# A planner's choice of engine for the query and key scaling, and 96 more constant bytes, in a one-core decoder layer

## The chip, the cores and the metric

The kernel runs on one core of one Trainium2 chip. The time is that of one execution on the device, in microseconds (us), first instruction to last with the launch around it; smaller is better. The engines are named as the profile names them: PE is TensorE's matmuls, PEld its loading of weights (the stationary operand), DVE is VectorE, ACT is ScalarE, POOL is GpSimd, SP the engine that only issues DMAs here.

## The reference, cut to what matters

One decoder layer on 1024 tokens of width 1024, all float32. Half of the mixer is stick-breaking attention (8 heads of 64), half a convolution; a gated feed-forward network follows.

```python
h = rms_norm(x, norm1_g)
q, k, v, glu_a, glu_b = split(h @ w_in)            # 5 x 512 columns
q = rms_norm(q.reshape(1, S, 8, 64), q_norm_g)     # each head's 64 values by themselves
k = rms_norm(k.reshape(1, S, 8, 64), k_norm_g)
attn = stick_breaking_attention(q, k, v)
c = causal_depthwise_conv(glu_a * sigmoid(glu_b), conv_dw_w, conv_dw_b)   # width 31
c = silu(layer_norm(c))
x = x + concat([attn, c]) @ w_out
h = rms_norm(x, norm2_g)
gate, val = split(h @ w_up)                        # 2 x 2816 columns
x = x + (silu(causal_dwconv3(gate)) * val) @ w_down
```

The diff touches the line `q = rms_norm(...)` and the one for `k`: for each token and head, 64 values are squared and summed, `rs` is the inverse root of their mean, and the 64 values are multiplied by `rs`. The gains are applied later.

## The kernel before, in words

**Precision.** Each large product is made of float32r operands split in a high and a low part: `mm3` (lines 324 to 327) issues three matmuls, high by high, high by low, low by high. The first operand of each is the stationary one (PEld loads 128 columns of it, 512 bytes in each partition), the second streams 512 columns past it.

**Stages.** First come the input projections, with the convolution and the attention beside them (one plan, lines 385 to 1409, up to about 437 us). Then the output projection's attention half, the second norm and the operands of the feed-forward network (a second plan, up to about 490 us). Then the up-projection: `up(f, A)` for 22 slices f of 128 channels, in one level of a Strassen-like scheme of seven products of 12 matmuls each (lines 1674 to 1700, 490 to 917 us). Last the down-projection `dn` (line 1844, 917 us to the end).

**Who sets the order.** `Plan` is a list scheduler written in Python that runs while the kernel is built. Each operation is added with a cost in ns for its engine, a due time (`key`), the operations that it comes after, and the buffer slots ("tokens") that it takes. `Plan.run` repeatedly takes the operation that can start first; then `in_order` makes each engine execute in exactly that order. So an engine waits in order: a late operation holds all that is queued behind it. If an operation's cost is given for several engines (a dict), the plan takes the engine on which it would end first: `start + cost`, where start is the later of its inputs and of the engine's being free. Key "DVE2" stands for DVE, and says that the operation shares a memory port with POOL: then the cost grows by as much as POOL's running operation holds on, at most by its own cost, and a POOL operation that runs beside it is put off likewise. Plain "DVE" costs know nothing of POOL.

**The operations around the change.** `project("qk0_", ...)` makes the queries and keys of heads 0 to 3, tile t of 128 tokens after tile t: 24 matmuls into a PSUM bank, 256 query and 256 key columns. `summed` (line 557) does the rest, for all eight tiles (`SUMMED_FIRST`), and for tiles 6 and 7 of heads 4 to 7 (`SUMMED`; tiles 4 and 5 there go through `normalized`, line 533):

1. copy out of PSUM on ACT or DVE (`copy_out`, line 528),
2. square on ACT (line 568),
3. sum over each 64 on DVE (line 577),
4. `rstd` on POOL (two small operations, lines 316 and 317),
5. `scale` on DVE: `tensor_tensor` with `rs` broadcast over 64 columns (line 573), two instructions of 128x256 for heads 0 to 3, one of 128x512 for heads 4 to 7. Its planned cost is 750.

`normalized` scales on ACT instead, in eight `activation` instructions of 128x64 each (line 547). `queries_keys` (tiles 0 to 3 of heads 4 to 7) scales out of PSUM on DVE, line 998; the diff leaves both alone.

**The convolution beside it.** For each of four channel groups c, DVE runs 31 dependent taps, one instruction each (`conv_a`, line 694, then `conv_b`, line 704). ACT makes 15 more scaled terms (line 718) that POOL adds up one after the other (line 721, three terms ahead at most). Three DVE operations (lines 734 to 736) join the three sums. When all four groups are joined (`conv_done`), PE turns them for the layer norm (`ln`, line 757), and those transposes stand in PE's queue between the query and key products. `double` (the queries' copy for the attention) waits for `conv_done` and for all eight scales.

**The next projection.** Tiles 4 to 7 of heads 4 to 7 use four pairs of weight rows `w_qk`. Each is loaded into one of two `raw` slots, copied to its high part on ACT (`hi_qk`, line 479), and subtracted for its low part on DVE or POOL (`lo_qk`, line 483). The parts lie in eight `whl` slots, six of which the weights of `qk0_` hold until the last tile has used them.

**Memory.** Pools without `side` are laid from the low end of each partition, those with `side="right"` from the high end. Low: the constants (`cst`, of which the unused tile `pad` is the first), small statistics, `mixp` (the convolution's sums, later the attention's result and the gates), `qkvp`, `convp`, and in the later stages `op` (tags xt, h2, v, m, t). High: weights (`whl`, `raw`), `h`, keys, the operands `b` of the up-projection, and all operands of the down-projection. In the kernel before, the large low tiles begin at 128 bytes past a multiple of 256, the high ones at 224, save two of the four `pad` tiles that hold the first weights of `glu` and `qk0_` (96). In the up-projection, the stationary operands of products 11 and 22 are low tiles (`op`, tags v and m; for f = 0, 11 and 12 in `mixp`), those of 12, S1, S2, S3, S4 high ones (`whl`); all moving operands are high.

Of the kernel before, what the change touches and what calls it, by code (L numbers as in the profile page):

```python
# [8 lines left out]
F32 = mybir.dt.float32  # L9
F32R = mybir.dt.float32r  # L10
BF16 = mybir.dt.bfloat16
AF = mybir.ActivationFunctionType
# [4 lines left out]
P = 128  # L17
# [45 lines left out]
class Plan:  # L63
# [32 lines left out]
    def add(self, cost, *args):  # L96
        if not isinstance(cost, dict):
            cost, args = {cost: args[0]}, (lambda eng, f=args[1]: f(),) + args[2:]
        op = Plan.Op()
        op.shares = "DVE2" in cost  # L100
        op.cost, op.emit, op.key = {e.rstrip("2"): c for e, c in cost.items()}, args[0], args[1]
        op.after = list(args[2]) if len(args) > 2 else []
        op.takes = list(args[3]) if len(args) > 3 else []
        op.end, op.engine, op.n, op.kb, op.dmas = None, None, len(self.ops), 512, 1
        self.ops.append(op)
        return op
# [101 lines left out]
def kernel(  # L208
# [21 lines left out]
    nc = tc.nc  # L230
# [28 lines left out]
    def const(shape, dt, name):  # L259
        return cst.tile(shape, dt, tag=name, name=name)  # L260


    const([P, 8], F32, "pad")

    small = ctx.enter_context(tc.tile_pool(name="small", bufs=1))
    mix_ctx = ExitStack()
# [47 lines left out]
    def rstd(dst, sums, scale):  # L314

        nc.gpsimd.tensor_scalar(dst, sums, scale, EPS, op0=ALU.mult, op1=ALU.add)
        nc.gpsimd.tensor_tensor(dst, dst, expo[:, :dst.shape[-1]], op=ALU.pow)
# [56 lines left out]
    def squares(token, name):  # L374
        return cp.tile([P, 512], F32, tag=f"squares{token.index}", name=name)
# [16 lines left out]
    add = plan.add  # L392

    def T(us):

        return (us - FIRST_STAGE) / 8.0

    def part_of(big_tile, i, words):
        return big_tile[:, i * words:(i + 1) * words]
# [124 lines left out]
    def copy_out(eng, pieces, ps):  # L524

        words = 512 // len(pieces)
        for n, piece in enumerate(pieces):
            (nc.scalar.copy if eng == "ACT" else nc.vector.tensor_copy)(piece, part_of(ps, n, words))

    def groups_of(pieces):  # L530
        return [part_of(piece, i, DH) for piece in pieces for i in range(8 // len(pieces))]
# [25 lines left out]
    def summed(name, d, o, m, to, at_):  # L557

        room, r, key = plan.token("squares"), plan.token("rs8"), T(at_)

        def groups(of):
            return of.rearrange("p (h d) -> p h d", d=DH)

        def square():
            d["sq"], d["rs"] = [small.tile([P, 8], F32, tag=f"{tag}8_{r.index}", name=f"{tag}_{name}") for tag in ("sq", "rs")]
            d["squares"] = squares(room, f"squares_{name}")
            for n, piece in enumerate(to()):
                nc.scalar.activation(part_of(d["squares"], n, 512 // len(to())), piece, AF.Square)

        def scale():  # L570
            for n, piece in enumerate(to()):
                g = 8 // len(to())
                nc.vector.tensor_tensor(groups(piece), groups(piece), d["rs"][:, n * g:(n + 1) * g].unsqueeze(2).to_broadcast([P, g, DH]), op=ALU.mult)

        m = add({"ACT": 600, "DVE": 690}, lambda eng: copy_out(eng, to(), d["ps"]), key, [m])
        a = add("ACT", 620, square, key, [m], [room, r])
        b = add("DVE", 690, lambda: nc.vector.tensor_reduce(d["sq"], groups(d["squares"]), axis=AX.X, op=ALU.add), key, [a])
        c = add("POOL", 1900, lambda: rstd(d["rs"], d["sq"], 1.0 / DH), key, [b])
        e = add("DVE", 750, scale, key, [c])
        room.users += [b]  # L580
        r.users += [e]
        o.users += [m]
        return e
# [524 lines left out]
    for h, half in [(h, half) for h in range(H) for half in range(2)]:  # L1108
        blk, c0, e = h // 4, (h % 4) * DH, h % 2
# [3 lines left out]
        qd, room, s, d = plan.token("qd"), plan.token("q"), plan.token("s"), {}  # L1113
# [31 lines left out]
        i = base  # L1145
        for g in (2 * half, 2 * half + 1):
            ws = []
            for u in range(2):
# [9 lines left out]
                d = {}  # L1158
# [46 lines left out]
            for sp in range(g + 1):  # L1205
                diag = sp == g
                s, th, tl, d = plan.token("s"), plan.token("thd" if diag else "th"), plan.token("tld" if diag else "tl"), {}
# [46 lines left out]
                c = add("DVE", 550 if diag else 680, low, k, [b], [tl])  # L1254
# [9 lines left out]
            if g % 2:  # L1264
                pa, pb = slice(e * DH, (e + 1) * DH), slice((1 - e) * DH, (2 - e) * DH)
                def dst(h=h, half=half, pa=pa):
                    return attn_row(h // 2)[pa, half * 512:(half + 1) * 512]

                def copied(dst=dst, pd=pd, pb=pb, h=h):
                    if h == 4 and len(attn) < 3:  # L1270
                        attn.append(True)
                        attn[1] = mixp.tile([P, S], F32, tag="attn_2", name="attn_last")
                    nc.scalar.copy(dst(), pd["po"].rearrange("p a t -> p (a t)")[pb, :])

                def summed(dst=dst, pd=pd, pa=pa):
                    nc.vector.tensor_tensor(dst(), pd["po"].rearrange("p a t -> p (a t)")[pa, :], dst(), op=ALU.add)

                a = add("ACT", 580, copied, i + 0.3, [last, prev_last] + conv_normed + (on_diagonal[0] if blk else []))
                b = add("DVE", 690, summed, i + 0.3, [a])
                po.users += [a, b]  # L1280
# [26 lines left out]
    def conv_half(n, k0, k1):  # L1307
# [4 lines left out]
        for t in range(4 * n, 4 * n + 4):  # L1312
# [19 lines left out]
            for nn in range(2):  # L1332
                o, r, m = plan.token("o"), plan.token("squares"), None
                cols = slice(nn * 512, (nn + 1) * 512)
                for kk in range(4):
                    def products(nn=nn, kk=kk, t=t, d=d, cols=cols, o=o):
                        if kk == 0:
                            d["ps", nn] = bank(o, [P, 512], f"op{t}_{nn}")
                        mm3(d["ps", nn], d["m"][:, 0, kk, :], d["m"][:, 1, kk, :], w_conv[kk][0][:, cols], w_conv[kk][1][:, cols], kk == 0, kk == 3)

                    m = add("PE", 685, products, k((nn * 4 + kk) / 8), [b, w_ready[kk]] + ([m] if m else []), [] if kk else [o])
                mr.users += [m]

                def out_of(nn=nn, t=t, d=d, r=r):
                    d["prod", nn] = squares(r, f"prod{t}_{nn}")
                    nc.scalar.copy(d["prod", nn], d["ps", nn])

                def summed(nn=nn, d=d, cols=cols):
                    nc.gpsimd.tensor_tensor(d["x"][:, cols], d["prod", nn], d["x"][:, cols], op=ALU.add)

                c = add("ACT", 600, out_of, k(nn / 2 + 0.5), [m], [r])
                f = add("POOL", 1290, summed, k(nn / 2 + 0.5), [c, xl])
                o.users += [c]
                r.users += [f]
                xr.users += [f]
# [66 lines left out]
    add = plan.add  # L1422
# [404 lines left out]
    for i in range(len(PAIRS)):  # L1827
        for n, name in enumerate(using if i else making):
# [4 lines left out]
            which, to = chain[name]  # L1833
            begins = name not in ("6", "7", "3")
            parts = made.pop((i, name))
            for s in range(4):
# [11 lines left out]
                if i == len(PAIRS) - 1 and name in whole_after:  # L1848
                    c = whole_after[name]
# [35 lines left out]
```

## Time and profile before

| | |
|---|---|
| runs | 1131.77, 1132.06, 1133.70 us; median 1132.06 |
| the profiled execution | 1132.88 us; its span, first to last instruction, 1130.7 us |
| share of the span busy | PE 97%, PEld 80%, DVE 80%, ACT 54%, POOL 49% |
| mean granted clock of PE | 0.992 |

The profile is of one execution. Its trace gives each instruction's start and length. Matmuls overlap in it: a 128x512 one is shown 0.39 us long, but they start 0.23 us apart, so starts are compared here rather than lengths. In the rows, `out<-in` are the program's names without numbers (`u_S` is any of the products S1 to S4, `u` one of 11, 12, 22), and a bracket at a row's end is the idle time before it and the instruction that ended it. Engine queues are in order; an engine that isn't the bound may idle at no cost.

### The profile page before, as it was taken

Reading aid. Unit: us, or ns where it says so; the run is one execution under the profiler, and the core shown is the slowest. Engines: PE = TensorE matmul, PEld = TensorE weight load, DVE = VectorE, ACT = ScalarE, POOL = GpSimd, SP = SyncE. Lnnn points to the kernel's source line nnn. Section 1 sums busy time; section 2 is a strip of 40 time slices with the busy share of each in tenths; the row PEclk is TensorE's granted clock in tenths of the full one; section 3 lists DMA queues with packets and bytes.
Section 4 is the critical chain, followed back from the end, with each engine's and each line's share of the span. In section 5 each row is a group of like instructions: output and inputs, shape, how many; then the busy total and the mean of one; then the engine's idle time right before and its main releaser. Section 6 shows DMA issues by size and latency. Waiting matters only on the chain.

```text
span 1130.7 us, 14860 instructions
## 1 busy us (share of the span) xinstructions
PE 1102.3 (97%) x5255; PEld 909.7 (80%) x5255; DVE 901.8 (80%) x1197; ACT 606.9 (54%) x1083; POOL 552.1 (49%) x487
## 2 busy tenths in 40 slices
PE   8999999798999999999999999999999999999998
PEld 5888888677888887878888888888888888888887
DVE  6498899769998887889887777778677678788885
ACT  6344564677887775654433333333333478776760
POOL 3165587567244532646432233223313189888770
PEclk8999999899999999999999999999999999999999
DMA  8110400332852314443223122222222382304303
GB/s 283 57 38 11 139 19 10 85 131 75 266 163 75 95 57 168 149 131 92 76 94 105 62 95 74 94 75 85 83 83 86 108 339 94 114 36 149 149 1 149
DMA packets 110232, 118.51 MB, mean 105 GB/s; under 512 B 21105, under 2 KB 89936, under 8 KB 110158
## 3 DMA queue, kind: packets, MB, share of 16 engines
q1 hardware_dynamic: 110014, 117.05, 31.4%
q8 instruction: 41, 0.67, 0.3%
q10 hardware_dynamic: 144, 0.52, 0.1%
q14 instruction: 33, 0.27, 0.1%
HBM read 82.95 MB, written 28.31 MB: 98 GB/s over the span
## 4 chain that ended last, share of the span: by engine, by line
PE 78%; DVE 11%; POOL 3%; ACT 3%; DMA 2%; issue 1%; SPq 0%; POOLq 0%; DVEq 0%; ACTq 0%
PE dn L1844 19%; PE u_S L326 7%; PE u_S L327 7%; PE u_S L325 7%; PE u L326 6%; PE u L325 5%; PE u L327 5%; PE po L1245 2%; POOL attn L721 2%; DVE conv_a L694 2%; PE wT L1217 2%; DVE nb L1190 2%; DVE conv_b L704 1%; PE opa L325 1%; PE opa L326 1%
## 5 line engine op out<-in xcount | busy, mean ns | idle before, releaser
L1844 PE MATMUL dn<-wd,wd 128*128 128x512 f32 x768 | 181.4, 389 | 0.0
L1844 PEld LDWEIGHTS dn<-wd,wd 128*128 128x128 f32 x768 | 144.1, 188 | 30.0
L326 PE MATMUL u_S<-bT,aS 128*128 128x512 f32 x264 | 102.8, 389 | 0.0
L327 PE MATMUL u_S<-bT,aS 128*128 128x512 f32 x264 | 102.7, 389 | 0.0
L325 PE MATMUL u_S<-bT,aS 128*128 128x512 f32 x264 | 102.4, 389 | 0.0
L1847 DVE TENSOR_TENSOR c<-dn,c 128x512 f32<-128x512 f32 x120 | 81.2, 685 | 25.4 <-PE dn L1844 25.0
L321 ACT CAST aS<-rawu 128x512 fp32r<-128x512 f32 x63 | 38.9, 620 | 96.8 <-PE u_S L327 68.1
L1749 ACT CAST wd<-rawd 128x512 fp32r<-128x512 f32 x128 | 72.6, 617 | 33.2 <-DMA rawd<-in_w_down_dram 9.0
L1190 DVE TENSOR_TENSOR_SCAN nb<-nb,one 128x128 f32<-128x128 f32 (+4 forms) x64 | 84.7, 1341 | 1.6 <-ACT nb L1176 1.4
L1591 POOL TENSOR_TENSOR s<-rawu 128x512 f32<-128x512 f32 x21 | 31.0, 1476 | 99.9 <-DMA rawu<-in_w_up_dram 98.6
L1748 ACT COPY whole<-rawd 128x512 f32<-128x512 f32 x110 | 63.4, 585 | 24.3 <-DVE wd L1750 11.6
L1750 DVE TENSOR_TENSOR wd<-whole,wd 128x512 fp32r<-128x512 f32 x90 | 59.9, 684 | 14.6 <-ACT wd L1749 8.0
L1597 POOL TENSOR_TENSOR rawu<-rawu 128x512 f32<-128x512 f32 x21 | 28.5, 1358 | 83.3 <-DVE a L322 83.3
L321 ACT CAST a<-rawu 128x512 fp32r<-128x512 f32 x63 | 39.0, 621 | 53.0 <-PE u_S L327 32.8
L326 PE MATMUL u<-b,a 128*128 128x512 f32 x168 | 66.6, 396 | 0.0
L1693 DVE SCALAR_TENSOR_TENSOR y<-gv,cols_a,y 128x1023 f32<-128x1023 f32 (+1 forms) x44 | 58.9, 1339 | 9.4 <-ACT y L1691 9.4
L325 PE MATMUL u<-b,a 128*128 128x512 f32 x168 | 66.2, 394 | 0.0
L327 PE MATMUL u<-b,a 128*128 128x512 f32 x168 | 65.6, 390 | 0.0
L322 DVE TENSOR_TENSOR a<-rawu,a 128x512 fp32r<-128x512 f32 x63 | 50.2, 797 | 16.1 <-ACT a L321 16.1
L326 PEld LDWEIGHTS u_S<-bT,aS 128*128 128x128 f32 x264 | 49.6, 188 | 10.7 <-issue 0.4
L1593 POOL TENSOR_TENSOR rawu<-s,rawu 128x512 f32<-128x512 f32 x21 | 32.2, 1536 | 53.0 <-DVE a L322 52.2
L325 PEld LDWEIGHTS u_S<-bT,aS 128*128 128x128 f32 x264 | 49.6, 188 | 10.3
(338 smaller groups left out, 3246.6 us busy)
## 6 DMA issues: line engine op xcount, KB each, us to landing
rawu<-in_w_up_dram SPq DMA_DIRECT2D x44, 512.0 KB
act_d<-y SPq DMA_DIRECT2D x22, 512.0 KB
rawd<-act_d SPq DMA_DIRECT2D x22, 512.0 KB
rawd<-in_w_down_dram SPq DMA_DIRECT2D x22, 512.0 KB
raw_qk<-in_w_in_dram SPq DMA_DIRECT2D x16, 256.0 KB
rawo<-in_w_out_dram SPq DMA_DIRECT2D x8, 512.0 KB
m<-conv_d SPq DMA_DIRECT2D x16, 256.0 KB
xt<-in_x_dram SPq DMA_DIRECT2D x8, 512.0 KB
```

Of the source, the lines that this page charges most:

```text
L321: nc.scalar.copy(hi, src)
L322: lo_engine.tensor_tensor(lo, src, f32(hi), op=ALU.subtract)
L325: nc.tensor.matmul(ps, a_hi, b_hi, start=first, stop=False)
L326: nc.tensor.matmul(ps, a_hi, b_lo, start=False, stop=False)
L327: nc.tensor.matmul(ps, a_lo, b_hi, start=False, stop=last)
L1190: nc.vector.tensor_tensor_scan(rev, rev, ones_of[0][:, :w], 0.0, op0=ALU.mult, op1=ALU.max)
L1693: nc.vector.scalar_tensor_tensor(y[:, j:], g[:, :S - j], par("fw", (KF - 1 - j) * NF + f), y[:, j:], op0=ALU.mult, op1=ALU.add)
L1748: nc.scalar.copy(whole, src)
L1749: nc.scalar.copy(t[:, 0], src)
L1750: lo_engine.tensor_tensor(t[:, 1], whole, f32(t[:, 0]), op=ALU.subtract)
L1844: nc.tensor.matmul(ps, a[:, tok], b, start=first and m == 0, stop=last and m == 2, skip_group_check=True)
L1847: nc.vector.tensor_tensor(sums[c][s], ps, sums[c][s], op=ALU.add)
```

## The change

`scale` in `summed` may run on ACT or on DVE, as the plan finds; on ACT in eight instructions of 64 columns, as in `normalized`. Its planned cost on DVE rises from 750 to 1900 and now counts POOL's hold of the port ("DVE2"); on ACT it is 1850. And the unused first constant grows from 8 words to 32 in each partition, which moves everything in the low pools up by 96 bytes: the large low tiles then begin at 224 of 256 bytes, as the high ones do. The constants behind it move as well (the identity for transposes from 160 to 0 of 256).

```diff
-    const([P, 8], F32, "pad")
+    const([P, 32], F32, "pad")
...
-        def scale():
+        def scale(eng):
+            if eng == "ACT":
+                for i, group in enumerate(groups_of(to())):
+                    nc.scalar.activation(group, group, AF.Copy, scale=d["rs"][:, i:i + 1])
+                return
             for n, piece in enumerate(to()):
                 g = 8 // len(to())
                 nc.vector.tensor_tensor(groups(piece), groups(piece), d["rs"][:, n * g:(n + 1) * g].unsqueeze(2).to_broadcast([P, g, DH]), op=ALU.mult)
...
-        e = add("DVE", 750, scale, key, [c])
+        e = add({"ACT": 1850, "DVE2": 1900}, scale, key, [c])
```

`groups_of(pieces)` (line 530) gives the eight slices of 64 columns; `Plan` and all other costs are as before.

## The prediction

> **What bounds the kernel now.** I read the page first, then the windows by stage, then PE's timeline where a window shows PE idle, then DVE's, POOL's and ACT's for the same stretch, last PE's starts in the up-projection.
>
> ```profile
> PE 1102.3 (97%) x5255; PEld 909.7 (80%) x5255; DVE 901.8 (80%) x1197; ACT 606.9 (54%) x1083; POOL 552.1 (49%) x487
> ...
> PE 78%; DVE 11%; POOL 3%; ACT 3%; DMA 2%; issue 1%; SPq 0%; POOLq 0%; DVEq 0%; ACTq 0%
> ```
>
> PE is busy 1102.3 of 1130.7 us and has 78% of the chain that ended last. So there are two ways to gain: the 28 us in which PE idles, and the pace of its matmuls.
>
> ```profile
> core 0: us, PE busy (x) PEld busy (x) DVE busy (x) ACT busy (x) POOL busy (x), PEclk, DMA share, GB/s
> 190.00:200.00 10.00, 8.17 (x38) 6.52 (x36) 9.79 (x13) 2.18 (x7) 6.91 (x6) 1.00 0.20 56
> 200.00:210.00 10.00, 5.41 (x22) 4.75 (x23) 9.90 (x18) 4.74 (x10) 4.04 (x5) 0.66 0.35 102
> ...
> 160.00:200.00 40.00, 38.17 (x169) 31.17 (x167) 39.22 (x51) 19.62 (x46) 30.71 (x28) 1.00 0.06 17
> 250.00:340.00 90.00, 83.81 (x545) 73.31 (x544) 87.20 (x108) 71.91 (x136) 43.92 (x47) 1.00 0.55 170
> 500.00:910.00 410.00, 410.00 (x1790) 335.60 (x1790) 310.62 (x372) 155.73 (x225) 138.94 (x94) 1.00 0.28 90
> ```
>
> Three stretches matter. From 160 to 200 DVE has no room (39.2 of 40 us), ACT half (19.6). From 198 to 207 PE has the largest hole of the program, and the granted clock falls to 0.66 behind it. From 500 to 910 PE never idles, so only its pace counts.
>
> ```profile
> 197.45 0.40 PE L327 MATMUL qk<-hi_qk,h_lo 128*128 128x512 f32 x1
> 197.69 0.49 PE L757 MATMUL ln<-ident_r,conv_out 128*128 128x128 f32 x3
> 204.59 2.15 PE L757 MATMUL ln<-ident_r,conv_out 128*128 128x128 f32 x9 [6.42 <-ACT q L528]
> 206.40 0.78 PE L325 MATMUL qk<-hi_qk,h_hi 128*128 128x512 f32 x1
> ...
> 207.82 0.41 PE L325 MATMUL qk<-hi_qk,h_hi 128*128 128x512 f32 x1
> ...
> 218.19 1.03 PE L783 MATMUL lnT<-ident_r,attn 128*128 128x128 f32 x8
> 218.98 0.48 PE L325 MATMUL qk<-hi_qk,h_hi 128*128 128x512 f32 x1
> ```
>
> PE ends the last tile of `qk0_`, turns the three channel groups of the convolution that are joined, and waits 6.42 us for the fourth. The bracket names ACT's copy out of PSUM, which ended at the same time, but the fourth group needs DVE's join (here two groups by line, then rows of DVE's timeline):
>
> ```profile
> L573 DVE TENSOR_TENSOR k<-k,rs_qk 128x256 f32<-128x256 f32 x8 | 9.7, 1217 | 0.0
> L573 DVE TENSOR_TENSOR q<-q,rs_qk 128x256 f32<-128x256 f32 x8 | 5.4, 671 | 0.1
> ...
> 193.36 0.42 DVE L573 TENSOR_TENSOR q<-q,rs_qk 128x256 f32<-128x256 f32 x1
> 193.70 2.62 DVE L573 TENSOR_TENSOR k<-k,rs_qk 128x256 f32<-128x256 f32 x1
> ...
> 201.98 0.68 DVE L734 TENSOR_TENSOR attn<-attn,conv_a 128x512 f32<-128x512 f32 x1
> ...
> 203.77 0.68 DVE L736 TENSOR_TENSOR conv_out<-attn,conv_b 128x512 f32<-128x512 f32 x1
> ...
> 205.50 0.42 DVE L573 TENSOR_TENSOR q<-q,rs_qk 128x256 f32<-128x256 f32 x1
> ...
> 211.88 0.42 DVE L573 TENSOR_TENSOR k<-k,rs_qk 128x256 f32<-128x256 f32 x1
> ```
>
> The join ends at 204.45, and PE starts 0.1 later. The scale takes 0.42 us when POOL is quiet, and up to 2.62 when POOL runs: the long one begins beside POOL's subtraction and ends with it:
>
> ```profile
> 192.40 1.09 POOL L721 TENSOR_TENSOR attn<-attn,attn_first 128x512 f32<-128x512 f32 x1
> 193.45 2.59 POOL L483 TENSOR_TENSOR lo_qk<-raw_qk,hi_qk 128x1024 fp32r<-128x1024 f32 x1
> ```
>
> Of 15.1 us of scales on DVE (9.7 + 5.4), the last four (0.42 each, 1.7) come behind the join. The other twelve take 13.4, less an overlap of 0.08 with each neighbour (193.36 + 0.42 against 193.70): 12.4 us of DVE's time ahead of the join. The old plan reckoned six times 0.75 there, 4.5. The other 8 us came unplanned, and PE's hole is about as large.
>
> **The scale, part by part.** Where does it go? The plan takes ACT unless ACT is free later than DVE by more than 50 ns and POOL's hold. With DVE 98% and ACT 49% busy between 160 and 200, I expect seven to nine of the ten operations on ACT. What an ACT scale costs:
>
> ```profile
> 220.21 2.02 ACT L547 ACTIVATE qk<-qk,rs_qk 128x64 f32<-128x64 f32 x8
> ```
>
> 2.02 us, close to the planned 1850, and ACT shows no wait for POOL. Six of them ahead of the join are 12.1 us in ACT's 20.4 idle ones: 79% busy. They are covered by ACT's waits for POOL; if these close, the third rival below has the price.
>
> What the hole costs today: 6.42 idle; then nine transposes in 1.81 (204.59 to 206.40), where eight take 0.79 later (218.19 to 218.98), so 0.92 too long; then three matmuls in 1.42 (206.40 to 207.82), against 0.68 at 0.227 apart, 0.74 too long. Sum 8.1 us. With 12.4 us taken from DVE the join would be at 192.1 by DVE alone. POOL's last addition ended at 193.49 (192.40 + 1.09), and three joins behind it at 2.5 us (201.98 to 204.45) give 196.0: ahead of PE's need at 197.7. So the hole closes, and next late are the weights (rows of the chain):
>
> ```profile
> 206.08 3.17 DMA raw_qk<-in_w_in_dram
> 209.32 1.06 ACT hi_qk L479
> 210.41 1.23 DVE lo_qk L483
> ```
>
> The second pair's slots become free four of eight steps (0.68 each) before the last tile's end at 197.7, at 195.0; its two parts take 1.06 + 1.23, to 197.3. Its raw slot then takes the fourth pair: 3.17 + 1.06 + 1.23 more, 202.8. PE wants that pair three times 1.36 after 197.7, at 201.8. So 1.0 us is late, of which transposes of the layer norm (0.1 each, sixteen at hand) can fill some: I keep 0.8. First term: 8.1 - 0.8 = **7.3 us**; bounds 0 and 8.1.
>
> For the rest of the first plan every order may change. The attention from 250 to 340 is bound by DVE (87.2 of 90 us) with 6.2 us of PE idle. Starting earlier moves it whole, since its inputs come from PE's products. The two late scales there:
>
> ```profile
> L573 DVE TENSOR_TENSOR qk<-qk,rs_qk x2: 1765/1772/1778, 243.6 to 260.6; 128x512 f32<-128x512 f32 x2
> ```
>
> On ACT they would relieve DVE of 3.5 us; left on DVE, nothing changes. A new order may lose as much as that. Second term: **0**, bounds 6 either way (all of that idle, gone or doubled).
>
> **The 96 bytes.** The starts of the seven products, f after f:
>
> ```profile
> 603.82 0.39 PE L325 MATMUL u_S<-b,aS 128*128 128x512 f32 x1
> ...
> 606.55 0.39 PE L325 MATMUL u<-bT,a 128*128 128x512 f32 x1
> ...
> 609.35 0.39 PE L325 MATMUL u<-b,a 128*128 128x512 f32 x1
> ...
> 612.15 0.40 PE L325 MATMUL u<-b,a 128*128 128x512 f32 x1
> ...
> 614.91 0.39 PE L325 MATMUL u_S<-bT,aS 128*128 128x512 f32 x1
> ...
> 617.63 0.39 PE L325 MATMUL u_S<-bT,aS 128*128 128x512 f32 x1
> ```
>
> Each row starts a product of 12 matmuls: S4 takes 2.73, 22 takes 2.80, 11 takes 2.80, 12 takes 2.76, S2 takes 2.72. The slow ones, 22 and 11, have their stationary operand in a low tile, 128 bytes past a multiple of 256; S2 and S4 have both operands at 224. 12 follows a slow product and looks like a recovery. If the low tiles begin at 224 too, all should take 2.72: 0.01 + 0.08 + 0.08 + 0.04 = 0.21 us for each f, and PE has no other wait there (410.00 of 410.00), so all of it is on the path. Some 21 of the 22 f (the first starts ragged): **4.4 us**. In the output projection every second tile has low stationary operands as well: 96 matmuls by 0.08/12 us are 0.6, on the path where PE is the bound; I take 0.3. Bounds for this edit: 0 and 5; a loss is excluded where both operands lie at 224, since S2 shows that case at the fast pace. Transposes against the moved identity are not shown by any row; some 600 of them, at the same 6.7 ns, bound that at 4 us either way, and I take 0.
>
> The Trainium skill speaks against this term: SBUF — State Buffer, "Who interferes with whom", gives PE two independent read ports, one for the moving operand and one for loading weights, and says that PE never waits on anyone. By it addresses cost nothing and the term is 0; the rows (2.80 against 2.72, by where the weights lie) disagree.
>
> **Sum.** 7.3 + 0 + 4.4 + 0.3 = 12.0 us. The profiled execution took 1132.9 (span 1130.7 and 2.2 around it), 0.8 above the median 1132.1; I take the gain off the median: **1120.1 us**.
>
> **Rivals.**
> - *The offset does nothing* (the pace comes from the tile's other users, not its address): 1132.1 - 7.3 = 1124.8. Against it: the pace is the same for every f. 0.10. By the page just named this is what happens.
> - *The hole stays*: the plan leaves most scales on DVE at the new price, or another wait, such as the weights, holds PE as long. 1132.1 - 4.7 = 1127.4. For it: the weights are late by 1 us anyway. Against it: ACT's idle half. 0.14.
> - *ScalarE becomes the bound*, from 160 to 200: a scale stands in its queue ahead of the terms that POOL adds, so POOL's chain lengthens. That chain has 8.5 us to spare (193.49 to 201.98). Ten scales are 20.2 us; if all delay it, 11.7 remain, less 4.7 from the offset: 7.0 slower, 1139.1. It turns slower once over 13.2 of the 20.2 us are on the path. Against it: the plan knows ACT's cost and fits it in. 0.07. The Trainium skill has the same direction: ScalarE: Activation LUTs, "Rules for kernel authors", says to multiply on VectorE rather than ScalarE. Undisturbed rows agree (0.84 against 2.02 us a tile), the disturbed one of 3.0 does not.
> - *The attention gives it back*: the new order adds twice the 6.2 us of idle: 1132.5. 0.08.
>
> **How the numbers follow.** The forecast keeps 0.61. A measurement of this kernel can tell about 0.2%, 2.3 us, from no change. Faster: 0.61 + 0.10 + 0.14 = 0.85; same 0.08; slower 0.07. The range takes the attention's 6 us downward, 1114.0, and upward the second rival and some of the attention's loss, 1130.0; the ends of the fourth and third rivals are left out.
>
> **What would show it.** Right: L547-like activations on ACT between 160 and 212 in place of L573; the join some 8 us earlier; no 6 us wait of `ln`; clock 1.00 there; 22, 11 and 12 at 2.72. Wrong: `ln` still waiting, now for POOL or ACT; 2.80 still in the up-projection; an attention whose PE idles more than before.

## The result, and the profile after

| | before | after |
|---|---|---|
| runs, us | 1131.71 to 1133.70, median 1131.91 | 1119.18 to 1121.80, median 1120.51 |
| ratio, with its 95% interval | | 0.9895 (0.9879 to 0.9910) |
| the profiled execution; its span | 1132.88; 1130.7 | 1119.90; 1118.1 |
| mean granted clock of PE | 0.992 | 0.998 |

The change makes the kernel 11.4 us faster by the medians; 1120.1 was forecast. First the engines' line and the chain's line of the page after, the answers to those quoted from before:

```profile
PE 1094.5 (98%) x5255; PEld 906.2 (81%) x5255; DVE 884.7 (79%) x1188; ACT 618.6 (55%) x1137; POOL 546.6 (49%) x485
...
PE 77%; DVE 9%; POOL 4%; ACT 4%; DMA 2%; issue 2%; SPq 0%; POOLq 0%; DVEq 0%; ACTq 0%
```

PE still bounds the kernel. The gain has two parts, and the two lines show both: PE is busy 7.8 us less with the same 5255 matmuls (1102.3 before), and idles 4.8 us less (span less busy: 28.4 before, 23.6 after). DVE gave work to ACT: 17 us off the one, 12 us onto the other.

The windows of the hole, of the attention's start and of the up-projection (columns: length, then busy times in us with instructions of PE, PEld, DVE, ACT and POOL, PE's granted clock, DMA share, GB/s):

```profile
160.00:200.00 40.00, 40.00 (x183) 33.06 (x182) 38.45 (x59) 30.27 (x88) 30.52 (x31) 1.00 0.12 31
200.00:210.00 10.00, 9.25 (x45) 7.08 (x44) 6.69 (x12) 6.87 (x27) 6.15 (x12) 1.00 0.52 143
240.00:250.00 10.00, 7.23 (x39) 4.90 (x40) 7.66 (x10) 9.62 (x20) 6.77 (x7) 1.00 0.40 133
500.00:900.00 400.00, 400.00 (x1767) 331.24 (x1766) 298.75 (x361) 152.01 (x218) 135.59 (x93) 1.00 0.29 93
```

From 160 to 200 PE no longer idles, and ACT went from 19.6 to 30.3 us. The window 200 to 210 has 9.25 where it had 5.41, and the clock stays at 1.00. In the up-projection PE is full as before, so that only its pace can have changed. Between 240 and 250 PE has 7.23 while ACT is at 9.62. That is no new loss: the attention starts 8 us earlier now, and in the kernel before the same stretch looked alike, PE 6.97 and ACT 8.70:

```profile
248.00:258.00 10.00, 6.97 (x40) 5.44 (x39) 8.87 (x13) 8.70 (x18) 7.74 (x10) 1.00 0.50 177
```

PE's timeline at the place of the old hole, then DVE's for the join:

```profile
196.53 0.40 PE L327 MATMUL qk<-hi_qk,h_lo 128*128 128x512 f32 x1
196.77 1.48 PE L761 MATMUL ln<-ident_r,conv_out 128*128 128x128 f32 x12
198.00 0.47 PE L325 MATMUL qk<-hi_qk,h_hi 128*128 128x512 f32 x1
```

```profile
192.40 0.43 DVE L577 TENSOR_TENSOR q<-q,rs_qk 128x256 f32<-128x256 f32 x1
192.74 0.42 DVE L577 TENSOR_TENSOR k<-k,rs_qk 128x256 f32<-128x256 f32 x1
193.65 0.69 DVE L581 TENSOR_REDUCE sq_qk<-squares_qk 128x8 f32<-128x512 f32 x1 [0.49 <-ACT squares_qk L568]
194.25 0.68 DVE L739 TENSOR_TENSOR conv_out<-conv_a,conv_out 128x512 f32<-128x512 f32 x1
194.84 0.68 DVE L740 TENSOR_TENSOR conv_out<-attn,conv_b 128x512 f32<-128x512 f32 x1
```

All twelve transposes follow the last tile at once. The join ends at 194.84 + 0.68 = 195.5, before PE's need at 196.8, and not at 204.5. Where the scales went (duration min, median and max in ns):

```profile
L573 ACT ACTIVATE q<-q,rs_qk x24: 331/335/353, 163.2 to 203.2; 128x64 f32<-128x64 f32 x24
L573 ACT ACTIVATE qk<-qk,rs_qk x8: 337/339/348, 253.6 to 255.3; 128x64 f32<-128x64 f32 x8
...
L577 DVE TENSOR_TENSOR q<-q,rs_qk x2: 418/422/426, 192.4 to 196.6; 128x256 f32<-128x256 f32 x2
L577 DVE TENSOR_TENSOR qk<-qk,rs_qk x1: 684/684/684, 234.2 to 234.2; 128x512 f32<-128x512 f32 x1
```

Seven of ten scales are on ACT (six of the eight first tiles, one of the two late ones). Of the twelve DVE instructions that cost 12.4 us ahead of the join, two are left, and they take 0.42 each.

PE's timeline in the up-projection, the starts of products 22, 11, 12 and S1:

```profile
616.38 0.39 PE L325 MATMUL u<-bT,a 128*128 128x512 f32 x1
...
619.10 0.39 PE L325 MATMUL u<-b,a 128*128 128x512 f32 x1
...
621.82 0.39 PE L325 MATMUL u<-b,a 128*128 128x512 f32 x1
...
624.54 0.39 PE L325 MATMUL u_S<-bT,aS 128*128 128x512 f32 x1
```

Each is 2.72 us behind the one before it. The landmarks of the two traces (starts of matmuls, before and after, us) say where the 12.6 us of span came from:

| stretch, up to | before | after | gained |
|---|---|---|---|
| first product of `qk0_` | 153.84 | 152.92 | 0.92 |
| last product of tiles 4 to 7 (the hole lies here) | 233.61 | 224.82 | 7.87 |
| the attention's first `z` product | 243.66 | 235.69 | -0.82 |
| the output projection's second part, `opa` | 437.15 | 429.51 | -0.33 |
| its last product | 487.45 | 479.16 | 0.65 |
| first product of the up-projection | 490.38 | 482.71 | -0.62 |
| its last product | 917.07 | 904.47 | 4.93 |
| end of the span | 1130.67 | 1118.11 | -0.04 |

Two of these rows belong together. Up to the first `z` product PE has no idle time behind tiles 4 to 7 in either kernel, but in the changed one eight transposes of the layer norm have moved from before that landmark to behind it (24 and 8 of the 32, where the kernel before has 32 and 0):

```profile
225.06 1.04 PE L761 MATMUL ln<-ident_r,conv_out 128*128 128x128 f32 x8
```

The next product starts 0.79 us later, at 225.85. So 0.8 of the 7.87 is not won and 0.8 of the -0.82 is not lost; over both rows the gain is 7.1 us (89.82 against 82.77).

### The profile page after: what moved, and what is told of

Its sections match the earlier page's. It is cut to its first block, busy times and chain, and to the rows that moved or that the text cites. A ratio compares the mean times of both kernels' runs of the same rounds, so it can differ in the third digit from the quotient of the medians.

```text
span 1118.1 us, 14908 instructions
## 1 busy us (share of the span) xinstructions
PE 1094.5 (98%) x5255; PEld 906.2 (81%) x5255; DVE 884.7 (79%) x1188; ACT 618.6 (55%) x1137; POOL 546.6 (49%) x485
## 4 chain that ended last, share of the span: by engine, by line
PE 77%; DVE 9%; POOL 4%; ACT 4%; DMA 2%; issue 2%; SPq 0%; POOLq 0%; DVEq 0%; ACTq 0%
PE dn L1848 19%; PE u_S L326 7%; PE u_S L327 7%; PE u_S L325 7%; PE u L327 5%; PE u L326 5%; PE u L325 5%; POOL attn L725 3%; PE po L1249 2%; PE wT L1221 2%; DVE nb L1194 2%; PE opa L325 1%; PE opa L327 1%; PE opa L326 1%; PE z L1172 1%
## 5 line engine op out<-in xcount | busy, mean ns | idle before, releaser
L1848 PE MATMUL dn<-wd,wd 128*128 128x512 f32 x768 | 181.5, 389 | 0.0
L326 PEld LDWEIGHTS u_S<-bT,aS 128*128 128x128 f32 x264 | 49.6, 188 | 11.4 <-POOL raws L1560 1.2
L325 PEld LDWEIGHTS u_S<-bT,aS 128*128 128x128 f32 x264 | 49.5, 188 | 10.7 <-ACT bT L1522 0.4
L327 PEld LDWEIGHTS u_S<-bT,aS 128*128 128x128 f32 x264 | 49.6, 188 | 10.3
L322 DVE TENSOR_TENSOR a<-rawu,a 128x512 fp32r<-128x512 f32 x63 | 47.0, 748 | 13.2 <-ACT a L321 13.2
```

What stands on the lines that cost most here:

```text
L322: lo_engine.tensor_tensor(lo, src, f32(hi), op=ALU.subtract)
L325: nc.tensor.matmul(ps, a_hi, b_hi, start=first, stop=False)
L326: nc.tensor.matmul(ps, a_hi, b_lo, start=False, stop=False)
L327: nc.tensor.matmul(ps, a_lo, b_hi, start=False, stop=last)
L1848: nc.tensor.matmul(ps, a[:, tok], b, start=first and m == 0, stop=last and m == 2, skip_group_check=True)
```

## The experiments

The theory: two separate edits add up. DVE spent 8 us too many on scales that met POOL, which held up the join and PE; the choice of ACT removes that. And PE is slow where its stationary operand lies at another residue of 256 bytes than the moving one; the pad removes that. The rivals: the order or the books do it rather than DVE's time; ScalarE becomes the bound; the address does nothing.

### The offset alone

```diff
 before.py
-    const([P, 8], F32, "pad")
+    const([P, 32], F32, "pad")
```

> The kernel before with the longer pad and nothing else. Main theory (two edits that add up: the offset speeds PE's matmuls where the stationary operand lay at another residue of 256 bytes than the moving one; the scales moved off DVE close PE's hole): the up-projection lasts 421.8 us instead of 426.7 from first to last product, as in the changed kernel, so 4.9 us come off; the first product of qk0_ starts up to 0.9 us earlier, but the join of the convolution still ends near 204.4, so that this part is swallowed by a longer hole (6.4 to 7.4 us). Time 1126 to 1127.3 us. Rival A (the up-projection became faster through something else in the new plan, such as when its weights arrive, and the address does nothing): 1131.9, products 22 and 11 stay at 2.80. Rival B (the offset also speeds the work on DVE and POOL that closes the hole): below 1123.

Measured: 1129.12 us, ratio to before 0.9957 (0.9940 to 0.9974), 4.1 us less by the medians. The up-projection lasted 422.3 us instead of 426.7, products 22, 11 and 12 all 2.72: its 4.4 us are the offset's, and rival A falls. PE's last tile, hole and restart of this kernel, then the first matmuls behind it:

```profile
197.70 0.49 PE L757 MATMUL ln<-ident_r,conv_out 128*128 128x128 f32 x3
204.54 0.87 PE L757 MATMUL ln<-ident_r,conv_out 128*128 128x128 f32 x3 [6.34 <-ACT q L528]
...
206.34 0.78 PE L325 MATMUL qk<-hi_qk,h_hi 128*128 128x512 f32 x1
...
209.05 0.63 PE L325 MATMUL qk<-hi_qk,h_hi 128*128 128x512 f32 x1
209.47 0.51 PE L326 MATMUL qk<-lo_qk,h_hi 128*128 128x512 f32 x1
209.82 0.40 PE L327 MATMUL qk<-hi_qk,h_lo 128*128 128x512 f32 x1
```

The hole is untouched (6.34 us), so the offset has no part in closing it, and rival B falls too. The time is 1.8 us above the forecast's upper end. The kernel before was 1.3 us higher in this comparison too; and in the profiled execution the stretch behind the hole, up to the end of tiles 4 to 7, took 1.4 us more than before. Most of that stands in these rows: matmuls are 0.43 apart until 209.47, where the kernel before was at full pace from 207.82. So in these two executions the cost of the hole differed with the moment at which PE's full pace came back.

### The choice of engine alone

```diff
 after.py
-    const([P, 32], F32, "pad")
+    const([P, 8], F32, "pad")
```

> The changed kernel with the old pad, so the choice of engine alone. Main theory: the hole of PE behind the last tile of qk0_ is gone (the first matmul of the next projection near 199 instead of 206.4, the join near 196 instead of 204.45), the attention's start gives 1.1 us back, and products 22 and 11 stay at 2.80: the gain is 12.5 less 4.9 and less up to 0.9, so 1125 to 1126 us. Rival A (the two edits need each other): less than 4 us faster, above 1128. Rival B (the scales are all of it): 1120.5.

Measured: 1125.22 us, 0.9930 (0.9912 to 0.9948), as the theory had it. PE's windows at the old hole:

```profile
190.00:200.00 10.00, 10.00 (x52) 8.42 (x51) 9.43 (x17) 7.28 (x22) 3.88 (x5) 1.00 0.07 15
200.00:210.00 10.00, 8.72 (x39) 6.41 (x39) 6.80 (x13) 5.51 (x20) 5.40 (x10) 1.00 0.67 180
```

The hole is gone, and products 22 and 11 take 2.80 as before. By medians the two single edits give 4.1 and 8.0 us, 12.1 together; the whole change gave 11.4 and, repeated, 13.1. They add up within the spread of the runs.

### The price alone

```diff
 after.py
-        e = add({"ACT": 1850, "DVE2": 1900}, scale, key, [c])
+        e = add({"DVE2": 1900}, scale, key, [c])
```

> The changed kernel, but the scale may run on DVE alone, at the new price of 1900 and with POOL's hold of the port in the plan's books. It tells the freed engine from the better books. Main theory (DVE's own time ahead of the join is what counts: 12.4 us of scales where undisturbed ones would take 5): the join comes later than PE needs it by at least a third of the old hole, 198.5 to 204; time 1122.5 to 1127. Rival (an order made with true prices is enough, since it keeps POOL's port operations away from the scales, so that each takes 0.42): join near 196, time 1119.5 to 1121.5, and the scales in the trace at 0.42 each.

Measured: 1138.29 us, 1.0044 (1.0029 to 1.0059): slower than before, outside both forecasts. Its scales by line, then its windows from 230 on:

```profile
L577 DVE TENSOR_TENSOR q<-q,rs_qk x8: 390/434/2609, 163.7 to 213.5; 128x256 f32<-128x256 f32 x8
L577 DVE TENSOR_TENSOR k<-k,rs_qk x8: 412/864/1519, 165.0 to 213.9; 128x256 f32<-128x256 f32 x8
```

```profile
230.00:240.00 10.00, 5.83 (x28) 3.83 (x26) 4.46 (x6) 7.69 (x19) 7.36 (x6) 0.74 0.26 105
240.00:250.00 10.00, 9.16 (x40) 7.98 (x40) 7.86 (x15) 4.57 (x9) 6.38 (x9) 0.58 0.52 157
250.00:260.00 10.00, 6.03 (x23) 3.75 (x21) 5.26 (x9) 7.82 (x16) 5.29 (x6) 0.76 0.23 91
```

The rival falls: with true prices in the books the scales still met POOL (up to 2.61 us; the twelve ahead of the join sum to 12.8 us, against 13.4 in the kernel before), and the join ended at 208.3, later than ever. The theory's direction holds, but not its place of payment: this plan put the transposes of the layer norm behind the next product, so PE had no hole at 197; it paid from 230 to 260 (21.0 of 30 us busy). Its first `z` product starts at 243.5 us, as in the kernel before (243.7), so up to there nothing was won; and the attention took 191.3 us from its first to its last `z` product, where the kernels before and after take 181. What the change brought is the second engine, not the better price.

### All ten scales on ScalarE

```diff
 after.py
-        e = add({"ACT": 1850, "DVE2": 1900}, scale, key, [c])
+        e = add({"ACT": 1850}, scale, key, [c])
```

> The changed kernel, but with all ten scales on ACT (the changed kernel puts seven there and three on DVE). Main theory (ACT has the room): three more scales of 2.02 us are 6 us more of ACT between 155 and 260 us, beside its waits for POOL; the hole stays closed, DVE gets 3 to 4 us free; time within 2 us of the changed kernel, 1118.5 to 1122.5. Rival (ScalarE becomes the bound, as the third rival of the prediction has it: its scales delay the terms that POOL adds): the join later by up to 6 us, PE waits there again, time 1123 to 1127.

Measured: 1122.00 us, 0.9902 (0.9887 to 0.9916), the join at 194.4, the hole closed. Three more scales cost nothing that shows beside the spread of the runs: ACT isn't the bound, and the rival falls.

### Scales out of PSUM on VectorE

For heads 0 to 3 the copy out of PSUM is left out; ACT squares and DVE scales from the bank, at the old price of 750. The diff shows the two main lines.

```diff
 after.py, in summed, for qk0_ only
+    nc.scalar.activation(d["squares"], d["ps"], AF.Square)
+    nc.vector.tensor_tensor(groups(piece), groups(part_of(d["ps"], n, 256)), d["rs"][:, 4 * n:4 * n + 4].unsqueeze(2).to_broadcast([P, 4, DH]), op=ALU.mult)
```

> The changed kernel, but the eight tiles of heads 0 to 3 are squared on ACT and scaled on DVE straight out of PSUM (two instructions of 128x256 a tile, planned at 750 as before), without the copy; the PSUM bank is held longer. It tells whether DVE was slow at the scale through its two operands in SBUF beside POOL. Main theory (DVE's 12.4 us ahead of the join were 5 us of work and 8 of contention; with one large operand in PSUM the contention goes): the scales take 0.4 to 0.6 us each even beside POOL, the join is near 196, PE's hole is closed; time 1118.5 to 1122.5. Rival (DVE is slowed by POOL wherever its operand comes from, since the output goes to SBUF): instructions up to 2.6 us again, the join after 200, time 1124 to 1128. A third way: the banks, held for the whole chain of square, sum, rstd and scale, hold up PE between 154 and 197: windows with PE under 9.5 of 10, time above 1123.

Measured: 1125.13 us, 0.9929 (0.9915 to 0.9944). The sixteen scales by line, then the windows of the attention's start:

```profile
L587 DVE TENSOR_TENSOR q<-qk,rs_qk x8: 410/418/425, 164.3 to 203.1; 128x256 f32<-128x256 f32 x8
L587 DVE TENSOR_TENSOR k<-qk,rs_qk x8: 406/415/416, 164.6 to 203.5; 128x256 f32<-128x256 f32 x8
```

```profile
240.00:250.00 10.00, 7.16 (x35) 4.79 (x34) 9.03 (x13) 9.02 (x18) 7.82 (x10) 0.97 0.47 160
250.00:260.00 10.00, 7.60 (x43) 6.12 (x42) 9.59 (x10) 7.87 (x20) 8.64 (x10) 0.86 0.47 132
260.00:300.00 40.00, 38.22 (x246) 33.12 (x247) 34.08 (x47) 28.15 (x55) 19.41 (x21) 1.00 0.48 158
```

This settles why DVE was slow. It is the same multiply by the same engine with POOL no less busy (32.6 us of 40 between 160 and 200, 30.7 in the kernel before), but with its large input in PSUM all sixteen take 0.41 to 0.43, 6.6 us in sum, where they took 15.1. The join ended at 195.3 and the hole closed with every scale of heads 0 to 3 on DVE. Nine of the sixteen began while one of POOL's additions ran, with up to 1.0 us of it left, and none was stretched. So this multiply meets POOL when both inputs lie in SBUF. The Trainium skill says this in SBUF — State Buffer, "Who interferes with whom": a DVE instruction with two SBUF inputs contends with POOL's reads, one with a single SBUF input doesn't. These rows agree. The theory's time failed, though, and the banks (the third way) are not the reason, since PE was at 10.00 in each window from 150 to 200. The loss is in the attention: 186.9 us from first to last `z` product, against 181.0.

### The late scales on VectorE

Two kernels ask where the attention loses. The first changes the two late scales of the changed kernel, the second does the same in the kernel that scales out of PSUM and prices that scale at 850.

```diff
 first kernel
-        e = add({"ACT": 1850, "DVE2": 1900}, scale, key, [c])
+        e = add({"ACT": 1850, "DVE2": 1900} if name.startswith("qk0_") else {"DVE": 750}, scale, key, [c])
 second kernel
-            e = add("DVE", 750, scale_ps, key, [c])
+            e = add("DVE", 850, scale_ps, key, [c])
-        e = add({"ACT": 1850, "DVE2": 1900}, scale, key, [c])
+        e = add({"DVE": 750}, scale, key, [c])
```

> The changed kernel, but the two late scales (tiles 6 and 7 of heads 4 to 7, at 234 and 253 us) go to DVE at the old price, 750; the eight of heads 0 to 3 choose as before. In the changed kernel one of the two is on ACT, which has 9.62 of 10 us between 240 and 250, while PE idles for 1.15 us more than in the kernel before. Main theory (that loss at the attention's start comes from ACT): ACT gets 2 us free at 253, PE idles about 1 us less between 240 and 262, time 1119 to 1120.5. Rival (the order of the attention matters more than one engine's load): the two DVE scales meet POOL and take up to 1.77 us each as in the kernel before, PE's idle time there is the same or larger, 1120.5 to 1123.5.

> The kernel that scales out of PSUM on DVE, with 850 as that scale's price (two instructions of 0.42 us) and with the two late scales on DVE at 750. It asks whether what that kernel lost (5.9 us more between the attention's first and last products than the changed kernel) hangs on the late scales' engine and on the order that follows. Main theory (the hole is closed in either way, and the rest is the order that the plan makes of the attention): the hole stays closed, the scales out of PSUM at 0.41 to 0.43 us, and if the attention is back at 181 us from first to last product, the time is 1117.5 to 1120.5. Rival (the longer hold of the PSUM banks, or the earlier start, costs the attention its time whatever is done with the late scales): 186 to 187 us there, 1123.5 to 1125.5.

> The changed kernel itself once more, as the measure for the two others on the same chip: 1119 to 1121.5 by either theory.

Measured on one chip: 1119.70 us, 0.9888 (0.9871 to 0.9906), for the first; 1119.39, 0.9880 (0.9864 to 0.9896), for the second; 1119.90, 0.9886 (0.9870 to 0.9902), for the changed kernel again. The three can't be told apart, so no version is shown to beat the changed kernel. PE's waits in the first, from 225 to 262 (total, times, longest), and in the changed kernel:

```profile
PE qk L325 <- DVE attn L1280: 1.6, 1, 1.6
PE z L1172 <- ACT nb L1180: 1.3, 1, 1.3
PE qT L1129 <- ACT conv_out L814: 0.8, 1, 0.8
```

```profile
PE z L1172 <- ACT nb L1180: 2.3, 3, 1.1
PE po L1249 <- DVE tl L1242: 0.8, 1, 0.8
PE qk L325 <- DVE attn L1280: 0.5, 1, 0.5
PE wT L1221 <- POOL nb L1199: 0.4, 1, 0.4
```

The late scales took 0.69 and 1.10 us on DVE. `z` waits 1.0 us less for ACT, but the next `qk` 1.1 more for DVE and `qT` 0.8 more for ACT's `conv_out`: PE's idle time has moved and hardly shrunk (3.7 us against 4.0). So the first theory there is not borne out, and neither is its premise: the kernel before waits 4.8 us in the same stretch, 8 us later (233 to 270), so PE did not idle more in the changed kernel. The 1.1 us that the attention seemed to give back are the eight transposes (0.8) and 0.3. The time, 0.2 us from the changed kernel's, decides nothing. In the second kernel the attention is back at 181.5 us with the same scales out of PSUM at 0.41 to 0.43: neither the banks nor the early start cost the 5.9 us, but the order that went with the other price and engine. Which operation of that order costs it was not isolated.

### Where the low tiles lie

Three kernels are the changed one with other pads: 16 words put the low tiles at 160 of 256 bytes, 24 words at 192; the third has 24 words and 8 unused words at the start of the right-hand pools, so that low and high tiles are both at 192.

```diff
-    const([P, 32], F32, "pad")
+    const([P, 16], F32, "pad")   (24 in the two others)
+    top = ctx.enter_context(tc.tile_pool(name="top", bufs=1, side="right"))   (third only)
+    top.tile([P, 8], F32, tag="top", name="top")
```

> The changed kernel with 16 words of pad: the large low tiles begin at 160 of 256 bytes, the high ones at 224. Main theory (PE is slow where the stationary operand lies at another residue of 256 than the moving one): products 22 and 11 take 2.80 us again, 12 about 2.76, the up-projection 426.7 us, time 1125 to 1126.5. Rival A (only 128 of 256 is slow): all products at 2.72, time 1120.5. Rival B (the cost grows with the distance of the two residues, 64 instead of 96 bytes): in between, products 22 and 11 near 2.77, time near 1123.5.

> The changed kernel with 24 words of pad: large low tiles at 192 of 256 bytes, high ones at 224, so 32 bytes apart. Main theory (equal residues are fast, unequal ones slow): 22 and 11 at 2.80, time 1125 to 1126.5. Rival A (only 128 is slow): 2.72 and 1120.5. Rival B (the cost grows with the distance): near 2.74 and 1121.5 to 1122.5.

> The kernel of the run with low tiles at 192, with 32 bytes more at the start of the right-hand pools, so that low and high tiles both begin at 192 of 256 bytes. Main theory (what counts is that both operands have the same residue): 22, 11 and 12 at 2.72 again, the up-projection 421.8 us, time 1120 to 1122 (two of the four tiles of the first weights then lie elsewhere, at most 0.5 us). Rival (224 itself is the fast place, or any place that isn't is slow): products whose operands are all high become slow too, each at 2.80, 22 times 7 times 0.08 or some 12 us slower than the changed kernel: 1130 to 1134.

Measured: 1122.36 us, 0.9901 (0.9884 to 0.9918), at 160; 1124.91, 0.9925 (0.9909 to 0.9941), at 192, 0.1 below the theory's range; 1120.20, 0.9888 (0.9870 to 0.9906), with both at 192. The starts of 22 and 11 in the three, in this order:

```profile
617.60 0.39 PE L325 MATMUL u<-bT,a 128*128 128x512 f32 x1
...
620.35 0.39 PE L325 MATMUL u<-b,a 128*128 128x512 f32 x1
```

```profile
618.39 0.39 PE L325 MATMUL u<-bT,a 128*128 128x512 f32 x1
...
621.19 0.39 PE L325 MATMUL u<-b,a 128*128 128x512 f32 x1
```

```profile
616.25 0.39 PE L325 MATMUL u<-bT,a 128*128 128x512 f32 x1
...
618.97 0.39 PE L325 MATMUL u<-b,a 128*128 128x512 f32 x1
```

22 takes 2.75 at 160, 2.80 at 192, and 2.72 with both at 192. So no residue is fast or slow by itself: 192 is slow beside 224 and fast beside 192. The theory's core holds and the rival of the third kernel falls. Its size fails at 160: 64 bytes apart cost 0.03 us a product, 32 and 96 apart 0.08. That is not rival B either, since the cost doesn't grow with the distance. What sets the size is not shown: 32 and 96 leave the same remainder by 64 and cost the same, 64 costs less and 0 nothing, but four points make no rule, and no run has a distance of 128.

## Why the prediction was right

**The hole.** Forecast 7.3, measured 7.1 from the first product of `qk0_` to the first `z` product (7.4 in the changed kernel's second profile); the 7.87 of the table's row has the eight moved transposes in it. The cause was right: contended scales on DVE, shown by the scales out of PSUM. The forecast of the join, 196.0, came out at 195.5, but by another way than argued. POOL's last addition was to stay at 193.5 and bound the join; it ended at 187.95. DVE bounded it still: of the 12.6 us that left its queue ahead of the join (13.4 less the 0.84 that stayed), part was filled by a second weight part `lo_qk` ahead of the join, four copies out of PSUM, and a wait for a square. "ACT 79% busy from 160 to 200" was 76% (30.27 of 40), seven of ten on ACT as forecast. The weights that were to be late by 0.8 us held PE 0.6 (`lo_qk`, at 203.3).

**The attention's 0.** Measured -0.3, from the first `z` product to the first of `opa` (193.5 us before, 193.8 after). That it came so near 0 is luck: the prediction worked out only bounds, no order of the attention, and two plans that closed or avoided the hole as well lost 6 and 10 us there (the scales out of PSUM, the price alone), the second more than the bound of 6 allowed.

**The 96 bytes.** Forecast 4.4, measured 4.2 in the 21 slices after the first (403.85 against 399.61 us), in the offset alone and in the whole change alike. The first slice gave 0.15 more in the offset alone and 0.7 in the whole change, where the granted clock stays at 1.00 (in the kernel before it is 0.50 from 491.3 to 494.5). The output projection gave 0.2 in the offset alone and 0.7 in the whole change, where 0.3 was forecast, but the wait behind it took 0.6 back. Not in the sum: the projections before `qk0_` gain some 0.5 us by the offset (from the start of the run of 24 matmuls near 49 us to the first product of `qk0_`, 103.9 and 104.0 us with it, 104.5 twice without); the rest of the 0.92 is the start, which in the changed kernel's second profile was 0.9 later again: a chance of that execution and no gain. Transposes against the moved identity cost nothing that shows. That 12 "looks like a recovery" from a slow product is not general: at 160 and 192 it took 2.72 behind a slow 11.

**The page against the rows.** By the rule of the Trainium skill (SBUF — State Buffer, "Who interferes with whom") that PE waits for nobody, the pad was worth nothing. No run here bears that out: the same product takes 2.72, 2.75 or 2.80 us by nothing but the place of its operands.

**The rivals.** None happened. "The hole stays" needed scales left on DVE, which the price alone made and which then cost more than before; "ScalarE becomes the bound" was refuted with all ten there, though the undisturbed prices do favour DVE (0.83 a tile out of PSUM against 2.02); what the multiply costs mattered less than what it delays.

## What to carry to other kernels

When one instruction takes several times as long at one place as at another, look at which engine starts and ends beside it before giving the work to a third engine; moving an input to PSUM may do as well. A planner with a true price but no second engine can do worse than one with a false price, so test the choice and the price apart. Lay both operands of such a matmul at the same residue of 256 bytes: the cost of each is small, but where PE never idles all of it is time. And before a later landmark is read as a loss, count what lies between the landmarks: here eight transposes had changed sides.

## What the runs showed of the hardware that was not expected

- The pace of 128x512 float32r matmuls with a fresh 128-column weight each depends on where the stationary operand begins relative to the moving one: 227 ns each with equal residues of 256 bytes, some 229 with 64 bytes between them, some 233 with 32 or 96 (2.72, 2.75 and 2.80 us for 12).
- DVE's multiply of two SBUF tensors was stretched from 0.42 to as much as 2.62 us beside POOL. The convolution's taps never were, though 52 of the 116 began while one of POOL's longer operations had over 0.3 us left. Their sums lie in PSUM (`bank`, lines 691 and 701; `mixp` holds POOL's sum alone), so only `cpad` is a large SBUF input. A scalar_tensor_tensor with both in SBUF (`y` and `gv`, lines 1680 and 1699) was stretched: 2.31 us beside POOL, 1.28 in the median. So here too the place of the inputs decides, and not the kind of instruction. Both are rows of the kernel before, the first by line; the 60 other taps took 0.74 to 0.76 as well:

```profile
L704 DVE SCALAR_TENSOR_TENSOR conv_b<-cpad,cols_b,conv_b x56: 742/756/757, 71.6 to 200.6; 128x512 f32<-128x512 f32 x56
...
526.59 2.31 DVE L1693 SCALAR_TENSOR_TENSOR y<-gv,cols_a,y 128x1023 f32<-128x1023 f32 x1
```

- After a hole of 6.4 us the matmuls ran 0.43 us apart for 3.2 us from PE's restart in the kernel before (204.6 to 207.8) and for 4.9 in the offset alone (204.5 to 209.5). The granted clock was 0.50 for some 6.8 us both times, and 1.00 on either side; only its place differs (columns as above):

```profile
201.02:207.85 6.83, 3.25 (x13) 3.00 (x14) 6.83 (x12) 4.06 (x9) 1.83 (x2) 0.50 0.20 56
202.95:209.65 6.70, 5.11 (x17) 4.47 (x18) 6.63 (x13) 2.49 (x7) 3.38 (x4) 0.50 0.45 120
```

  The Trainium skill (TensorE: Matmul & The Clock Gate, "Part 1: The HAM clock gate") has the full clock come back after a busy window of about 3.4 us, and has the windows run free, so that the wait depends on the moment. Both executions fit that: 6.8 us are about two such windows, and by an estimate from these rows and that figure the second of them begins near 204.5 in the one, as PE restarts, and near 206.3 in the other, 1.8 us behind the restart.
